# Reading seven latent tiles of the first mixer's input from a second, feature-major copy of x

## The chip, the cores and the metric

The kernel runs on one core of a Trainium2 chip. The metric is the device time of one execution in microseconds (us). The engines are named as in the profile: PE is TensorE (its weight loads are the separate row PEld), DVE is VectorE, ACT is ScalarE, POOL is GpSimd, and SP is SyncE, whose queue issues nearly all DMA transfers of this kernel.

## The reference, cut to what matters

The program is a two-layer trunk of a generator over 1024 latent tokens and 256 context tokens with 1024 features. Layer 0 mixes by windowed attention, layer 1 by gated linear attention; each is followed by an MLP. The change touches only the input of layer 0's mixer: a norm over each token's features, then a scale and a shift per feature, then the projection to q, k and v.

```
def rms_norm(x, gain):
    xf = x.astype(jnp.float32)
    y = xf * lax.rsqrt(jnp.mean(xf * xf, axis=-1, keepdims=True) + NORM_EPS)
    return (y * gain.astype(jnp.float32)).astype(x.dtype)

def modulate(x, gain, shift, scale):
    return rms_norm(x, gain) * (1 + scale) + shift
...
        h_lat = modulate(x_lat, g_pre_mix[i], m_lat[0], m_lat[1])
        h_ctx = modulate(x_ctx, g_pre_mix[i], m_ctx[0], m_ctx[1])
...
    def project(h):
        T = h.shape[1]
        qkv = h @ w_qkv
```

The norm's factor is one number per token; gain, scale and shift are one number per feature. The shifts and scales are themselves a product of the condition vector with `w_mod`.

## The kernel before, in words

**Tiles.** Tokens are cut into ten tiles of 128: tiles 0 and 1 are context, 2 to 9 latent. A tile of rows has tokens on the 128 partitions and 1024 features along them. The projection needs the other layout, features on partitions, since PE contracts over partitions: eight blocks of 128 features by 128 tokens. Every product is made from fp32 numbers split into a high and a low part (`split`, L212 on ACT and L213 on DVE), in three matmuls (`mm3`, L228 to L230). One token tile takes 8 blocks times 3 column groups times 3 = 72 matmuls into q (two groups, one PSUM pair) and kv (one group).

**From rows to operands.** `x_in` (L482) loads a tile of rows by SP's queue. `normed` squares and sums it on ACT (`rms`, L235), makes the factor in two small POOL steps (`rstd`, L241 and L242) and scales the rows on DVE (L430). `modulated` transposes the eight blocks on PE (L442), which land in two PSUM banks of four blocks, applies scale and shift block by block on ACT (L461, even blocks) and DVE (L463, odd blocks) while copying to SBUF, and splits each half into the operands `ah` and `al`. After the matmuls `qkv_out` copies q (L606) and kv (L610) out of PSUM on ACT, `rotary` turns them on DVE and POOL, and `q_out` (L615) stores q to DRAM by SP's queue.

**Order of the work.** `first_tiles` handles the two context tiles while the weights arrive; at its last block (`k == KT - 1`) it calls `pre(2)`, which makes the operands of tile 2 and, like every `pre(i)`, loads the rows of tile i + 2. Rows of tiles 2 and 3 are loaded at block 5 of that loop. Up to here the code stands in a region in which every engine takes its instructions in the order in which they are written. Behind it the tile framework's planner orders each engine's instructions by its own simulated times, and each engine then executes them strictly in that order, SP's queue too: a DMA that waits for its data holds back all that stand behind it. In this part tiles 2 to 6 go through the loop with `qkv_tile`, and tiles 7 to 9 through `qkv_apart`, where PE's order alone is written out and carries pieces of the context tiles' attention (L827 to L854) and, at place 11, the transposes of the next tile. Between the blocks of tiles 2 to 5, `next(mods)` does one step of the sums for later modulation vectors: a load of `w_mod` (L297), a multiply-add on DVE (L308, L310) and, at a vector's end, small PE matmuls (L326). A finished vector goes to DRAM (L335) and comes back as a column per feature (L348, used in L349). After tile 9 the latent attention begins, then the output projection and the MLP.

**Buffers.** One pool of 45 SBUF slots of 4 KB per partition (`u`) serves weights, rows, operands, q and kv; a load waits until a slot is free. PSUM gives four banks (`ps1`) and two bank pairs (`ps2`).

Of the kernel before, what the change touches and what calls it, by code (L numbers as in the profile page):

```python
# [11 lines left out]
F32 = mybir.dt.float32  # L12
F32R = mybir.dt.float32r
AF = mybir.ActivationFunctionType
ALU = mybir.AluOpType
# [3 lines left out]
P = 128  # L19
D = 1024  # L20
KT = D // P
SEQ = 1024
CTX = 256
NC_T = CTX // P
NL_T = SEQ // P
NT = NC_T + NL_T
# [138 lines left out]
class Backbone:  # L165
# [267 lines left out]
    def modulated(self, xn, l, which, s, dst=(), put=None):  # L433

        nc = self.nc
        G, S = self.pre[l, which]
        pts = {}

        def turn(q):
            for k in range(4):  # L440
                kk = 4 * q + k
                nc.tensor.transpose(pts[q][:, P * k : P * (k + 1)], xn[:, P * kk : P * (kk + 1)], self.ident)  # L442

        if self.tight:
            both = self.ps2("xt")
            for q in range(2):
                pts[q] = both[:, 512 * q : 512 * (q + 1)]
                turn(q)
        for q in range(2):
            if not self.tight:  # L450
                pts[q] = self.ps1("xt")
                turn(q)
            pt = pts[q]
            h = None if put else self.half("h").rearrange("p (k t) -> p k t", k=4)
            for k in range(4):
                kk = 4 * q + k
                to = put(kk) if put else h[:, k, :]
                src = pt[:, P * k : P * (k + 1)]
                sc, sh = G[:, s, kk : kk + 1], S[:, s, kk : kk + 1]
                if k % 2 == 0:  # L460
                    nc.scalar.activation(to, src, AF.Identity, scale=sc, bias=sh)  # L461
                else:
                    nc.vector.tensor_scalar(to, src, sc, sh, ALU.mult, ALU.add)  # L463
            for k0, k1, hi, lo in dst:
                a, b = max(k0, 4 * q), min(k1, 4 * q + 4)
                if a < b:
                    self.split(h[:, a - 4 * q : b - 4 * q, :], hi[:, a - k0 : b - k0, :], lo[:, a - k0 : b - k0, :])

    def post_norm(self, y, x, grow):

        nc = self.nc
        r = self.rms(y, self.junk)
        o = self.u(s="xo")
        nc.vector.tensor_tensor(o, y, grow, op=ALU.mult)
        nc.vector.scalar_tensor_tensor(o, o, r, x, ALU.mult, ALU.add)
        return o
# [984 lines left out]
    def gla_running(self, head, g, logs):  # L1461
# [5 lines left out]
        for d, lg in enumerate(logs):  # L1467
            run = self.half("run")[:, :w]
            r3 = run.rearrange("p (c t) -> p c t", t=P)
            l3 = lg.rearrange("p (c t) -> p c t", t=P)  # L1470
            tot, mid = self.tot[head][:, d, self.chunks(g)], self.mid[head][:, d, self.chunks(g)]
            if d == 0:
                nc.vector.tensor_tensor_scan(run, self.reset[:, :w], lg, 0.0, ALU.mult, ALU.add)
                nc.vector.tensor_copy(mid, r3[:, :, 63])
                nc.vector.tensor_copy(tot, r3[:, :, P - 1])
            else:
                nc.vector.memset(run[:, 0:1], 0.0)
                nc.vector.tensor_tensor_scan(
                    run[:, 1:w], lg[:, 0 : w - 1], self.reset[:, 1:w], 0.0, ALU.add, ALU.mult
                )  # L1480
                nc.vector.tensor_copy(mid, r3[:, :, 64])
                nc.vector.tensor_tensor(tot, r3[:, :, P - 1], l3[:, :, P - 1], op=ALU.add)
            nc.vector.tensor_tensor(r3, r3, mid.unsqueeze(2).to_broadcast([P, nch, P]), op=ALU.subtract)
            if g > 0 or d == 0:
                ex = self.u((P, 2, 512), s="ex")
            up, down = (ex[:, 0, :], ex[:, 1, :]) if g else (None, ex[:, d, :w])
            sgn = 1.0 if d == 0 else -1.0
            nc.scalar.activation(down, run, AF.Exp, scale=-sgn / TAU)
            if g > 0:
                nc.scalar.activation(up, run, AF.Exp, scale=sgn / TAU)  # L1490
            res.append((up, down))
# [189 lines left out]
    def run(self):  # L1681
        nc, t = self.nc, self.t
        self.gm, self.pre = {}, {}
        self.q, self.oT = {}, {}
        groups = [[0, 1], [2, 3, 4, 5], [6, 7, 8, 9]]


# [1 line left out]
        h = Acts(self, [[0, 1]])  # L1689

        def pre(i):
            h = Acts(self, [[i]])
            dst = h.pieces(i)
            xn = self.normed(xs.pop(0), dst[0][2])
            self.modulated(xn, 0, 0, self.stream(i), dst)
            if i + 2 < NT:
                xs.append(self.x_in(i + 2))
            return h

        with self.tc.manual_schedule():  # L1700
            self.consts()
            xs = self.xs
            pq, pkv, h = self.first_tiles(xs, h, pre)
# [21 lines left out]
        for i in range(2, NT - 3):  # L1725
            nxt = pre(i + 1)
            does = {k: lambda: next(mods) for k in (0, 2, 5)} if i < NT - 4 else {}
            if i == 4:
                self.kc = [self.u((P, KVH, CTX), F32R, s="kc") for _ in range(2)]
                for k, fs in ((3, self.keys(0)), (4, self.keys(1)), (6, self.queries(self.qs, 0, 0))):  # L1730
                    does[k] = lambda fs=fs: [f() for f in fs]
            self.qkv_tile(i, h, lambda k: does.get(k, int)())
            h = nxt
            self.rotary(i)
            self.q_out(i)
        ctx = self.ctx_rounds()
        with self.tc.manual_schedule(engines={mybir.EngineType.PE}):
            for i in range(NT - 3, NT):
                does = {}
                for n in (1, 5, 9, 13, 17, 21):  # L1740
                    if ctx:
                        does[n] = [ctx.pop(0) for _ in range(2 if (i, n) == (NT - 1, 17) else 1)]
                if i + 1 < NT:
                    nxt = Acts(self, [[i + 1]])
                    dst = nxt.pieces(i + 1)
                    xn = self.normed(xs.pop(0), dst[0][2])
                    if i + 3 < NT:
                        xs.append(self.x_in(i + 3))
                    does.setdefault(11, []).append(lambda: self.modulated(xn, 0, 0, self.stream(i + 1), dst))
                else:  # L1750
                    ks = {}

                    def begin():
                        ks["a"], ks["b"] = self.lat_keys()
                        self.q_back(NC_T)
                        ks["a"][0](), ks["b"][0]()

                    does.setdefault(7, []).append(begin)
                    does.setdefault(11, []).append(lambda: ks["a"][1]())
                    does.setdefault(12, []).append(lambda: (ks["b"][1](), ks["a"][2](), ks["a"][3]()))  # L1760
                    does.setdefault(14, []).append(
                        lambda: [f() for f in self.queries(self.qs, NC_T, 0) + ks["b"][2:4]]
                    )
                    for n in (19, 24):
                        does.setdefault(n, []).append(lambda: next(latents))
                self.qkv_apart(i, h, i < NT - 1, does)
                h = nxt
                if i < NT - 2:
                    self.rotary(i)
                    self.q_out(i)  # L1770
            assert not ctx
# [327 lines left out]
```

## Time and profile before

| | |
|---|---|
| median of three runs | 2597.32 us (2594.55 to 2599.63) |
| the profiled execution's own time | 2597.13 us |
| its span | 2595.4 us |
| matmuls on PE in all | 13451 |
| transposes of L442 in this stage | 64 (63.8 to 204.1 us), eight for each of tiles 2 to 9 |
| data moved by DMA in all | 351.36 MB, 135 GB/s on average |

How to read the lines that the prediction quotes. A line of the timeline gives the start and the length in us from the span's start, the engine (SPq is SP's queue), the kernel's line, the operation, what it writes and reads, shapes, how many were merged into the line, and in brackets how long the engine had stood idle and what released it. A line of the waits gives who waited for whom, the total in us, the times and the longest. A line of the groups gives busy us in all and the mean ns of one, then the idle time before it. Matmuls overlap, so their lengths say less than the distance between two starts.

### The profile page before, as it was taken

How to read it: one execution, taken by the hardware profiler on the slowest of the kernel's cores; microseconds unless marked ns; L12 is line 12 of the kernel's file. 1: busy time of each engine (PE TensorE's matmuls, PEld its weight loads, DVE VectorE, ACT ScalarE, POOL GpSimd, SP SyncE). 2: the span in 40 equal slices, each digit the busy share in tenths (PEclk: the TensorE clock that was granted, in tenths of full speed). 3: DMA queues.
4: the chain of work that ended last, by engine and by line, in shares of the span. 5: the costliest groups of instructions: out<-in, count | busy, mean ns of one | idle time of the engine just before them, and what ended most of it. 6: DMA issues, size and time to landing. Idle time of an engine off the chain costs nothing. (4 is left out here: it accounts for less than half of the span.)

```text
span 2595.4 us, 36179 instructions
## 1 busy us (share of the span) xinstructions
PE 2529.4 (97%) x13451; PEld 2105.8 (81%) x13451; DVE 1703.1 (66%) x2587; ACT 1255.6 (48%) x2350; POOL 435.2 (17%) x720
## 2 busy tenths in 40 slices
PE   7999999999999999999999999999999999999998
PEld 6778888788888888888877888888887888878886
DVE  4775888657766665858777635646658656566676
ACT  3345777644645454433435545334436555545333
POOL 0354666421000000000002213312310000000002
PEclk9999999999999999999999999999999999999999
DMA  9210121322455675737255331103331544567474
GB/s 313 90 66 25 34 59 51 99 89 78 146 157 164 187 224 161 274 130 277 80 173 200 101 91 49 33 18 97 112 103 46 191 142 156 167 244 238 159 232 159
DMA packets 240801, 351.36 MB, mean 135 GB/s; under 512 B 35000, under 2 KB 133584, under 8 KB 240624
## 3 DMA queue, kind: packets, MB, share of 16 engines
q1 hardware_dynamic: 238032, 339.60, 40.4%
q0 software_dynamic: 2592, 9.44, 0.9%
q8 instruction: 106, 1.74, 0.3%
q14 instruction: 71, 0.58, 0.1%
HBM read 273.41 MB, written 75.56 MB: 134 GB/s over the span
## 5 line engine op out<-in xcount | busy, mean ns | idle before, releaser
L229 PE MATMUL p<-ol,oh 128*128 128x512 f32 x896 | 349.8, 390 | 0.2
L230 PE MATMUL p<-oh,ol 128*128 128x512 f32 x896 | 346.5, 390 | 0.0
L228 PE MATMUL p<-oh 128*128 128x512 f32 x896 | 329.3, 392 | 8.6 <-ACT oh L212 5.4
L241 POOL TENSOR_SCALAR rs<-ss 128x1 f32<-128x1 f32 (+1 forms) x78 | 27.7, 355 | 1627.1 <-ACT later L235 1446.4
L213 DVE TENSOR_TENSOR ol<-wh,oh 128x1024 fp32r<-128x1024 f32 x128 | 153.8, 1221 | 81.8 <-ACT oh L212 80.5
L228 PEld LDWEIGHTS p<-oh 128*128 128x128 f32 x896 | 168.3, 188 | 47.0 <-ACT oh L212 8.6
L212 ACT CAST oh<-wh 128x1024 fp32r<-128x1024 f32 x128 | 131.5, 1050 | 154.5 <-DVE wh L1216 34.9
L229 PEld LDWEIGHTS p<-ol,oh 128*128 128x128 f32 x896 | 168.6, 188 | 36.4 <-DVE ol L213 1.5
L230 PEld LDWEIGHTS p<-oh,ol 128*128 128x128 f32 x896 | 168.5, 188 | 35.1
L310 DVE SCALAR_TENSOR_TENSOR ma<-wm,cT,ma 128x1024 f32<-128x1024 f32 x112 | 147.6, 1346 | 40.8 <-DMA wm<-in_w_mod 40.6
L212 ACT CAST oh<-k 128x1024 fp32r<-128x1024 f32 x96 | 98.0, 1055 | 128.1 <-DMA k<-in_w_mlp_out 61.7
L213 DVE TENSOR_TENSOR wi<-wi,wi 128x512 fp32r<-128x512 f32 x176 | 116.7, 687 | 49.7 <-ACT wi L212 45.9
L1046 ACT COPY s<-pa 128x512 f32<-128x512 f32 x96 | 56.0, 584 | 175.4 <-PE pa L230 175.3
L771 POOL TENSOR_SCALAR pr<-pr,den 128x640 f32<-128x640 f32 (+2 forms) x160 | 126.3, 803 | 33.4 <-DVE den L769 21.7
L213 DVE TENSOR_TENSOR ol<-k,oh 128x1024 fp32r<-128x1024 f32 x96 | 113.7, 1220 | 23.6 <-ACT oh L212 20.1
L212 ACT CAST wi<-wi 128x512 fp32r<-128x512 f32 x176 | 103.9, 615 | 33.9 <-DMA hd<-h 15.1
L228 PE MATMUL y<-woh,oh 128*128 128x512 f32 x288 | 115.0, 400 | 2.5 <-ACT woh L212 1.3
L759 ACT ACTIVATE pr<-pr,nm 128x640 f32<-128x640 f32 (+1 forms) x128 | 102.5, 802 | 28.3 <-DVE nm L754 26.9
L230 PE MATMUL y<-woh,ol 128*128 128x512 f32 x288 | 113.2, 394 | 1.3 <-DVE ol L213 1.3
L229 PE MATMUL y<-wol,oh 128*128 128x512 f32 x288 | 112.6, 392 | 0.1
L230 PE MATMUL rp<-wgh,al 128*128 128x512 f32 x288 | 112.0, 390 | 0.0
L229 PE MATMUL rp<-wgl,ah 128*128 128x512 f32 x288 | 112.0, 390 | 0.0
(385 smaller groups left out, 6696.5 us busy)
## 6 DMA issues: line engine op xcount, KB each, us to landing
wm<-in_w_mod SPq DMA_DIRECT2D x96, 512.0 KB
hd<-h SPq DMA_DIRECT2D x80, 512.0 KB
wh<-hd SPq DMA_DIRECT2D x144, 256.0 KB
wh<-in_w_mlp_out SPq DMA_DIRECT2D x144, 256.0 KB
wi<-in_w_mlp_in SPq DMA_DIRECT2D x64, 512.0 KB
k<-hd SPq DMA_DIRECT2D x80, 256.0 KB
k<-in_w_mlp_out SPq DMA_DIRECT2D x80, 256.0 KB
x<-in_x SPq DMA_DIRECT2D x16, 512.0 KB
```

The costliest lines, as they stand in the source:

```text
L212: self.nc.scalar.copy(hi, src)
L213: self.nc.vector.tensor_tensor(lo, src, hi.bitcast(F32), op=ALU.subtract)
L228: mm(out, a[0], b[0], start=start, stop=False, skip_group_check=onto)
L229: mm(out, a[0], b[1], start=False, stop=False, skip_group_check=onto)
L230: mm(out, a[1], b[0], start=False, stop=stop, skip_group_check=onto)
L241: nc.gpsimd.tensor_scalar(r, ss, inv_n, EPS, ALU.mult, ALU.add)
L310: nc.vector.scalar_tensor_tensor(acc[s], raw, c, acc[s], ALU.mult, ALU.add)
L759: nc.scalar.activation(pr, pr, AF.Exp, bias=nm[:, e : e + 1], scale=-1.0, accum_out=sums[:, e : e + 1])
L771: nc.gpsimd.tensor_scalar(pr, pr, den[:, e : e + 1], 0.0, ALU.mult, ALU.add)
L1046: nc.scalar.copy(s["s", j], s["pa"])
```

## The change

The host adds one more input, `in_x_t`: for each of the eight latent tiles the same numbers with features on partitions (partition, feature block, token). The latent tiles 3 to 9 no longer go through `normed` and `modulated` here. Their rows are still loaded, but only for `row_scale`: sum of squares, factor, then the 128 factors are written to a DRAM tile by SP and read back by SP so that every partition holds all 128 of them (`rb`). `xt_in` loads the turned tile, and `from_turned` multiplies it on DVE by the factors (two instructions of four blocks), applies scale and shift in SBUF on ACT and DVE in turn, and splits the halves as before. Tile 2 keeps the old way. `ahead(i)` replaces the load of rows i + 2: it issues the turned tile i + 1 and the rows and factor of tile i + 2 (for i = 2 first the factor of tile 3). In the three tiles with PE's order written out, `from_turned` is called at place 11, where the transposes were.

```
+    def row_scale(self, i, x):
+        r = self.rms(x, x)
+        d = self.dp.tile([P], F32, name=self.nm("rd"))
+        self.nc.sync.dma_start(d.rearrange("(p o) -> p o", o=1), r)
+        self.rb[i] = self.sm.tile([P, P], F32, tag="rb", name=self.nm("rb"), bufs=3)
+        self.nc.sync.dma_start(self.rb[i], d.partition_broadcast(P))
+
+    def xt_in(self, i):
+        self.xt[i] = self.u((P, KT, P), s="xt")
+        self.nc.sync.dma_start(self.xt[i], self.t["x_t"][i - NC_T])
+
+    def from_turned(self, i, dst):
+        nc = self.nc
+        xt, r = self.xt.pop(i), self.rb.pop(i)
+        G, S = self.pre[0, 0]
+        for q in range(2):
+            ks = slice(4 * q, 4 * q + 4)
+            nc.vector.tensor_tensor(xt[:, ks, :], xt[:, ks, :], r.unsqueeze(1).to_broadcast([P, 4, P]), op=ALU.mult)
+            for k in range(4 * q, 4 * q + 4):
+                x, sc, sh = xt[:, k, :], G[:, 0, k : k + 1], S[:, 0, k : k + 1]
+                if k % 2 == 0:
+                    nc.scalar.activation(x, x, AF.Identity, scale=sc, bias=sh)
+                else:
+                    nc.vector.tensor_scalar(x, x, sc, sh, ALU.mult, ALU.add)
+            for k0, k1, hi, lo in dst:
+                a, b = max(k0, 4 * q), min(k1, 4 * q + 4)
+                self.split(xt[:, a:b, :], hi[:, a - k0 : b - k0, :], lo[:, a - k0 : b - k0, :])
...
         def pre(i):
             h = Acts(self, [[i]])
             dst = h.pieces(i)
-            xn = self.normed(xs.pop(0), dst[0][2])
-            self.modulated(xn, 0, 0, self.stream(i), dst)
+            if i == NC_T:
+                xn = self.normed(xs.pop(0), dst[0][2])
+                self.modulated(xn, 0, 0, self.stream(i), dst)
+            else:
+                self.from_turned(i, dst)
+            ahead(i)
+            return h
+
+        def ahead(i):
+
+            if i == NC_T:
+                self.row_scale(i + 1, xs.pop(0))
+            if i + 1 < NT:
+                self.xt_in(i + 1)
             if i + 2 < NT:
-                xs.append(self.x_in(i + 2))
-            return h
+                self.row_scale(i + 2, self.x_in(i + 2))
...
                     nxt = Acts(self, [[i + 1]])
                     dst = nxt.pieces(i + 1)
-                    xn = self.normed(xs.pop(0), dst[0][2])
-                    if i + 3 < NT:
-                        xs.append(self.x_in(i + 3))
-                    does.setdefault(11, []).append(lambda: self.modulated(xn, 0, 0, self.stream(i + 1), dst))
+                    ahead(i + 1)
+                    does.setdefault(11, []).append(lambda: self.from_turned(i + 1, dst))
...
+    arrays["in_x_t"] = np.ascontiguousarray(inputs["x"][0].reshape(NL_T, P, KT, P).transpose(0, 3, 2, 1))
```

More of the change, by code (lines that the diff above doesn't have):

```diff
@@ L1683, in run @@
         self.gm, self.pre = {}, {}
-        self.q, self.oT = {}, {}
+        self.q, self.oT, self.xt, self.rb = {}, {}, {}, {}
         groups = [[0, 1], [2, 3, 4, 5], [6, 7, 8, 9]]
```

## Prediction

> **What bounds the kernel now.** First the page's top and busy times, then the busy time by stretch, then the list of what TensorE waited for between 64 and 215 us, then the timeline at the places that list names.
>
> ```profile
> span 2595.4 us, 36179 instructions
> PE 2529.4 (97%) x13451; PEld 2105.8 (81%) x13451; DVE 1703.1 (66%) x2587; ACT 1255.6 (48%) x2350; POOL 435.2 (17%) x720
> 60.00:220.00 160.00, 152.77 (x779) 123.99 (x780) 114.53 (x157) 64.60 (x153) 74.86 (x100) 0.98 0.22 75
> 220.00:530.00 310.00, 302.02 (x2716) 257.16 (x2715) 231.12 (x483) 219.39 (x561) 177.40 (x331) 0.99 0.20 56
> PE xt L442 <- DVE x L430: 3.3, 1, 3.3
> PE sc L827 <- ACT pr L835: 1.7, 1, 1.7
> PE q L228 <- ACT q L606: 1.4, 1, 1.4
> ```
>
> TensorE (PE) is busy 97% of the span. In the stretch that the change touches (60 to 220 us; columns: length, PE, weight loads, DVE, ACT, POOL busy, granted clock, DMA share, GB/s) it stands 7.2 us of 160. Three named waits stand out there, and the longest, 3.3 us, is a transpose that waits for the normed rows. So what takes instructions off PE here ends the stage sooner by their issue time, as long as their successors are ready. The next stretch is just as full of PE (302 of 310), so time saved at 220 us should reach the end.
>
> The profiled execution took 2597.13 us by its own time, 1.7 more than its span; the median of the three runs is 2597.32 (2594.55 to 2599.63). I sum against 2597.1. About 0.2%, 5.2 us, is what a measurement of this kernel can tell from no change.
>
> **Removed: 56 transposes.** Each of the seven tiles loses eight matmuls of line 442.
>
> ```profile
> 74.43 1.03 PE L442 MATMUL xt<-ident,x 128*128 128x128 f32 x8
> 75.22 0.48 PE L228 MATMUL kv<-wkvh,ah 128*128 128x512 f32 x1
> 75.53 0.40 PE L229 MATMUL kv<-wkvl,ah 128*128 128x512 f32 x1
> 75.77 0.39 PE L230 MATMUL kv<-wkvh,al 128*128 128x512 f32 x1
> 76.00 0.39 PE L228 MATMUL kv<-wkvh,ah 128*128 128x512 f32 x1
> ```
>
> The first column is the start. Ordinary matmuls follow each other every 0.23 us (75.77 to 76.00). From the first transpose to the second matmul behind it (74.43 to 75.53) is 1.10; less one interval, eight transposes cost 0.87 us. Seven tiles: 6.1 us, all on PE.
>
> **Removed: the wait at one transpose.**
>
> ```profile
> 134.62 0.39 PE L230 MATMUL q<-wqh,al 128*128 128x512 f32 x1
> 138.34 1.76 PE L442 MATMUL xt<-ident,x 128*128 128x128 f32 x8 [3.33 <-DVE x L430]
> 139.75 0.77 PE L228 MATMUL kv<-wkvh,ah 128*128 128x512 f32 x1
> 142.03 0.39 PE L230 MATMUL kv<-wkvh,al 128*128 128x512 f32 x1
> 142.26 0.39 PE L228 MATMUL kv<-wkvh,ah 128*128 128x512 f32 x1
> 140.00:160.00 20.00, 20.00 (x90) 16.49 (x90) 15.31 (x18) 5.94 (x11) 10.01 (x9) 0.95 0.48 168
> ```
>
> PE stood 3.33 us and then ran slowly, which the granted clock of 0.95 shows too: eight transposes in 1.41 us (138.34 to 139.75) instead of 0.79 (74.43 to 75.22), and the five matmuls to 142.03 in 2.28 instead of five times 0.23. The stall's price is 3.33 + 0.62 + 1.13 = 5.1 us. The matmuls behind it (kv) belong to a tile whose operands were ready; only the place of the transposes in PE's order made them wait. With no transpose there, nothing of the new path stands in that place, so I take the 5.1 as gone. What is late next is the operand at a tile's first matmul.
>
> **Work that moves on the other engines.**
>
> ```profile
> L430 DVE TENSOR_SCALAR x<-x,rs 128x1024 f32<-128x1024 f32 x8 | 9.4, 1181 | 3.0 <-DMA wm<-in_w_mod 1.5 <-POOL rs L242 1.5
> L213 DVE TENSOR_TENSOR al<-h,ah 128x512 fp32r<-128x512 f32 x16 | 10.6, 686 | 2.4 <-ACT ah L212 2.3
> L709 DVE TENSOR_TENSOR t<-q,rope 128x512 f32<-128x512 f32 x6 | 6.3, 1054 | 0.5 <-ACT q L606 0.5
> L310 DVE SCALAR_TENSOR_TENSOR ma<-wm,cT,ma 128x1024 f32<-128x1024 f32 x112 | 147.6, 1346 | 40.8 <-DMA wm<-in_w_mod 40.6
> L548 DVE TENSOR_SCALAR h<-xT,G,S 128x256 f32<-128x256 f32 x4 | 1.7, 413 | 0.1
> L461 ACT ACTIVATE h<-xt,S,G 128x128 f32<-128x128 f32 x32 | 13.8, 459 | 50.6 <-PE xt L442 41.3 <-DVE h L463 8.0 <-DVE kv L712 0.8
> L463 DVE TENSOR_SCALAR h<-xt,G,S 128x128 f32<-128x128 f32 x32 | 12.4, 406 | 13.5 <-ACT h L461 13.2
> ```
>
> (Columns: busy in all, mean ns of one, idle before it.) On DVE one scaling of 1181 ns per tile goes and two 128x512 multiplications with two tensors come: 686 ns each by the nearest row, 1054 by the slowest of this size, a rotary one. That is 0.2 to 0.9 us more per tile, at most 6.5 in seven, against 45 us in which DVE stands in this stretch: nothing on the path. The VectorE: DVE Perf Modes page of the Trainium skill (section on why `tensor_tensor` can't do 2×_2P) speaks against the exchange: a two-tensor fp32 operation runs at half the rate of a one-tensor scaling from SBUF. The rows agree in kind, and if DVE set the pace the rule would take back about that 0.2 to 0.9 us per tile. Shift and scale stay eight instructions a tile, now from SBUF; 256 columns cost 413 ns there, so 128 cost no more than the 406 and 459 now, and I take no difference. Their mutual waits (13.2 and 8.0 us) may shrink, which is cover only. Square sums and POOL's two small steps stay, a tile earlier.
>
> DMA gets seven tiles of 512 KB more, 3.7 MB. The DMA share of 0.22 at 75 GB/s leaves room for several times that: nothing. Two row loads now go out at 49.60, just behind the last weight; they will no longer stand there.
>
> ```profile
> 49.12 0.38 SPq L220 DMA_DIRECT2D wqr<-in_attn_w_qkv  x1
> 49.60 0.86 SPq L482 DMA_DIRECT2D x<-in_x  x2
> 56.14 1.05 ACT L212 CAST wqh<-wqr 128x1024 fp32r<-128x1024 f32 x1 [2.54 <-DMA wqr<-in_attn_w_qkv]
> 60.10 0.79 PE L228 MATMUL q<-wqh,ah 128*128 128x512 f32 x1 [2.43 <-ACT ah L212]
> ```
>
> That weight landed seven us after its issue, and PE's 2.43 us at 60.10 hang on it. If the loads behind it slow it, up to those 2.4 us could be won; if the queue is served in order, nothing. I take nothing, since other loads close up behind it, and keep the 2.4 for the low end.
>
> **Added: the way through DRAM.** The factor is written to DRAM and read back to all partitions. No such pair stands in the trace; the nearest one is a modulation vector's:
>
> ```profile
> 980.48 0.54 SPq L335 DMA_DIRECT2D md<-mrow  x2
> 981.97 0.39 SPq L348 DMA_DIRECT2D G<-md  x1
> 984.41 0.17 DVE L349 TENSOR_TENSOR G<-G,bcol 128x8 f32<-128x8 f32 x1 [0.18 <-DMA G<-md]
> x1d<-xo POOLq DMA_DIRECT2D x10, 512.0 KB, 3.1
> ```
>
> 1.5 us from the write's issue to the read's, 3.9 to the use. Between the two SP stands, and everything behind it on SP's queue with it: the next turned tile, the next rows, modulation weights and stores of q. A full tile lands in 3.1. From the Square to the factor the chain takes 2.1 us:
>
> ```profile
> 70.04 1.10 ACT L235 ACTIVATE ah<-x 128x1024 fp32r<-128x1024 f32 x1
> 72.05 0.63 ACT L212 CAST ah<-h 128x512 fp32r<-128x512 f32 x1 [0.48 <-DVE h L463]
> 72.17 0.75 DVE L430 TENSOR_SCALAR x<-x,rs 128x1024 f32<-128x1024 f32 x1 [0.15 <-POOL rs L242]
> 68.36 0.50 PE L228 MATMUL q<-wqh,ah 128*128 128x512 f32 x1 [1.41 <-ACT q L606]
> ```
>
> The DMA: Bandwidth & Descriptors page (specifications table) of the Trainium skill adds that writes below 512 bytes are done as read-modify-write; the factor's are 4 bytes each, and no run here shows what that costs.
>
> The one tight place is the first tile of the new path, tile 3. By the order written in the diff its Square comes after the last cast of tile 2. That cast was at 72.05 with the Square ahead of it; without, about 71. So Square 71.6, factor 73.7, read issued 75.2, turned tile issued 75.7 behind it, landed 78.8. Two multiplications, four scalings on two engines, cast and subtraction (0.69 + 0.9 + 0.62 + 0.69) make the first half ready at about 82. PE comes to it when tile 2's 72 matmuls from 68.36 at 0.23 are through: 84.9. That leaves under 3 us, and two of DVE's modulation steps (1346 ns each, line 310) in front would use them up. Every later tile has its factor and its turned tile a whole tile (16.6 us) ahead.
>
> **Sum.** 6.1 + 5.1 removed; new waits between 0 and 5.1 (a wait at tile 3 as dear as that of 138.34), of which I take the middle, 2.5, because the margin of 3 us is near what two DVE steps cost. Forecast: 2597.1 − 11.2 + 2.5 = 2588.4 us.
>
> **Rivals.**
> - *The wait only moves.* The order on the engines is planned anew after the first tiles, and a wait like that of 138.34 comes back elsewhere, since DVE and POOL are as loaded as before. For it: two other waits, of 1.7 and 1.4 us, stand in the same stretch. Against: PE depended on the normed rows there through the transposes alone. Then 2597.1 − 6.1 = 2591.0, and with tile 3's 2.5 too 2593.5.
> - *Slower: SP's queue brings the operands late.* A factor's write waits in SP's queue for its Square, and a Square stands in ACT's queue behind the copy of q out of PSUM, which waits for PE (190.72, 191.64):
>
> ```profile
> 190.72 1.03 ACT L606 ACTIVATE q<-q 128x1024 f32<-128x1024 f32 x1 [0.89 <-PE q L230]
> 191.64 1.05 ACT L235 ACTIVATE ah<-x 128x1024 fp32r<-128x1024 f32 x1
> SPq L615 <- DVE q L712: 111.5, 6, 42.3
> ```
>
> SP already stands 111.5 us at six stores of q. If turned tiles are issued behind both, tiles come late one after another at 5.1 us each. It decides from three of the seven on (11.2 / 5.1 = 2.2); with four, 2597.1 − 11.2 + 20.4 = 2606.3. Against it: two tiles of lead.
> - *It doesn't reach the end.* The attention that follows waits for something else; then about 2597. Against it: PE's 302 of 310 us.
>
> **How the numbers follow.** Forecast 0.52, wait only moves 0.27, slower by SP 0.14, doesn't reach the end 0.07. Forecast and the lower edge of the second rival are faster by over 0.2%: 0.52 + 0.05. Within 0.2%: 0.22 + 0.07. Slower 0.14. The forecast's own range is 2583.5 (2597.1 − 11.2 − 2.4) to 2591 (with all 5.1 of new waits). The whole range goes from that, rounded to 2583, up to 2601, just short of three late tiles (2601.2), and leaves out most of the slow case and a few hundredths below.
>
> **What would show it.** Right: eight transposes of line 442 left before 220 us instead of 64; no PE wait for line 430 after tile 2; the stage's last q copy earlier by 8 to 11 us and the same lead at the end. Wrong: PE waits for `ah` or `al` of a new tile behind the new multiplication, above all near 85 us; or SP standing before a turned tile's load for longer than a tile; or the lead gone between 220 and 530 us.

## The result and the profile after

The changed kernel takes 2635.94 us (median of five runs, 2632.54 to 2638.56) against 2597.32: 1.0146 times as long (95% interval 1.0132 to 1.016). Its profiled execution took 2637.8 us, with a span of 2636.1, which is 40.7 more than before.

The page's top, then the busy time by stretch (the columns as in the prediction):

```profile
span 2636.1 us, 36127 instructions
PE 2528.5 (96%) x13395; PEld 2102.9 (80%) x13395; DVE 1699.2 (64%) x2594; ACT 1255.3 (48%) x2350; POOL 443.2 (17%) x720
```

```profile
60.00:220.00 160.00, 108.82 (x445) 84.23 (x445) 84.60 (x123) 43.85 (x88) 60.46 (x55) 0.84 0.39 107
220.00:530.00 310.00, 301.56 (x2643) 258.88 (x2644) 230.50 (x475) 215.08 (x575) 183.75 (x344) 0.98 0.14 40
200.00:220.00 20.00, 1.65 (x3) 0.83 (x3) 8.86 (x17) 5.37 (x15) 9.05 (x11) 0.50 0.19 68
```

The 56 transposes are gone (13451 matmuls have become 13395). Over the whole span PE now idles 107.6 us (2636.1 − 2528.5), 41.6 more than before. Between 60 and 220 us alone PE stands 51.2 us and not 7.2, which is 44.0 more; the next stretch idles as before, and a little is won back behind it. PE's busy total has fallen by only 0.9 us, although transposes worth 6.1 were removed: what is left runs longer, at a granted clock of 0.84 in the stretch. What PE waited for between 55 and 300 us:

```profile
PE sc L857 <- ACT pr L865: 16.9, 1, 16.9
PE q L230 <- DVE al L213: 10.6, 2, 10.4
PE kt L672 <- POOL k L667: 10.6, 2, 7.4
PE q L228 <- ACT ah L212: 9.8, 3, 6.7
PE q L228 <- ACT q L636: 5.4, 1, 5.4
```

These five lines make 53 us (2.4 of them, at 60.56, stood in the kernel before too), and three different engines are named in them. What holds up all three shows in the list of SP's waits (48 to 280 us) and in SP's own timeline:

```profile
SPq L474 <- POOL rs L242: 63.3, 7, 21.2
SPq L476 <- DMA rd<-rs: 53.5, 7, 8.6
```

```profile
71.25 0.33 SPq L474 DMA_DIRECT2D rd<-rs  x1
79.10 0.33 SPq L476 DMA_DIRECT2D rb<-rd  x1
79.52 0.38 SPq L480 DMA_DIRECT2D xt<-in_x_t  x1
...
90.64 0.33 SPq L474 DMA_DIRECT2D rd<-rs  x1
91.06 0.39 SPq L512 DMA_DIRECT2D x<-in_x  x1
91.54 0.38 SPq L297 DMA_DIRECT2D wm<-in_w_mod  x1
99.72 0.33 SPq L476 DMA_DIRECT2D rb<-rd  x1
```

L474 writes the 128 factors of a tile, 4 bytes from each partition; L476 reads them back and has to wait until the write is confirmed. That took 7.85 us at 71.25 and 9.08 at 90.64; in all seven tiles it is between 7.5 and 9.1. SP stands through it, and everything behind it on its queue too: tile 3's turned copy is not issued before 79.52. The loads that were issued behind the second write, ahead of the read, fare no better. The busy time by stretch, finer (last column: GB/s):

```profile
73.00:79.00 6.00, 6.00 (x28) 4.98 (x27) 0.00 (x0) 0.10 (x1) 0.00 (x0) 1.00 0.00 0
94.00:96.00 2.00, 2.00 (x11) 1.62 (x10) 0.00 (x0) 0.00 (x0) 0.00 (x0) 1.00 0.61 37
98.00:99.70 1.70, 1.70 (x9) 1.43 (x8) 0.00 (x0) 0.00 (x0) 0.00 (x0) 1.00 0.36 19
102.00:104.00 2.00, 2.00 (x10) 1.65 (x10) 0.09 (x1) 1.27 (x3) 0.03 (x1) 1.00 0.85 279
```

During the first write nothing else moves (0 GB/s), so no other transfer explains the 7.85 us. During the second, loads of 512 KB crawl (37 and 19 GB/s in the two stretches shown), and once it is confirmed they run at 279. How PE comes to feel it, in the timeline:

```profile
86.29 1.29 DVE L488 TENSOR_TENSOR xt<-xt,rb 128x512 f32<-128x512 f32 x2 [16.31 <-DMA xt<-in_x_t]
87.02 1.65 ACT L492 ACTIVATE xt<-xt,S,G 128x128 f32<-128x128 f32 x4 [13.93 <-DVE xt L488]
90.27 0.80 PE L228 MATMUL q<-wqh,ah 128*128 128x512 f32 x1 [6.67 <-ACT ah L212]
91.29 0.63 PE L230 MATMUL q<-wqh,al 128*128 128x512 f32 x1
91.72 0.63 PE L228 MATMUL q<-wqh,ah 128*128 128x512 f32 x1
...
102.73 1.06 ACT L235 ACTIVATE x<-x 128x1024 f32<-128x1024 f32 x1 [12.00 <-DMA x<-in_x]
103.92 1.42 DVE L308 TENSOR_SCALAR ma<-wm,cT 128x1024 f32<-128x1024 f32 x2 [12.37 <-DMA wm<-in_w_mod]
118.23 1.28 DVE L310 SCALAR_TENSOR_TENSOR ma<-wm,cT,ma 128x1024 f32<-128x1024 f32 x1 [5.43 <-DMA wm<-in_w_mod]
119.44 0.69 DVE L213 TENSOR_TENSOR al<-xt,ah 128x512 fp32r<-128x512 f32 x1
120.18 0.79 PE L230 MATMUL q<-wqh,al 128*128 128x512 f32 x1 [10.39 <-DVE al L213]
```

At 86.29 DVE multiplies tile 3 after standing 16.31 us for the turned copy, and PE has stood 6.67 when it starts at 90.27. At 120.18 PE stands 10.39 us for a subtraction on DVE whose inputs were there; a modulation step ahead of it on DVE (118.23) had waited for its `w_mod`, which came late. ACT's and POOL's queues jam in the same way behind the Square of the rows (102.73). The longest wait, 16.9 us at 220.88, goes back there too: ACT's scalings of tile 9 waited 14.63 us for DVE's multiplication, and that had waited 8.69 for the turned copy. Behind a stall PE also runs at half speed: from 91.29 to 91.72 a matmul takes 0.43 us in place of 0.23, as it does from 90.27 to 93.00. The Trainium skill (TensorE: Matmul & The Clock Gate, Part 1) says that PE falls to half its clock after being idle and needs some 3.4 us of work to come back; the rows agree in kind, with 2.7 us here.

### The profile page after: what moved, and what is told of

Same layout as the page of the kernel before. It is cut to its first block, busy times and chain, and to the rows that moved or that the text cites. A ratio compares the mean times of both kernels' runs of the same rounds, so it can differ in the third digit from the quotient of the medians.

```text
span 2636.1 us, 36127 instructions
## 1 busy us (share of the span) xinstructions
PE 2528.5 (96%) x13395; PEld 2102.9 (80%) x13395; DVE 1699.2 (64%) x2594; ACT 1255.3 (48%) x2350; POOL 443.2 (17%) x720
## 5 line engine op out<-in xcount | busy, mean ns | idle before, releaser
L212 ACT CAST oh<-k 128x1024 fp32r<-128x1024 f32 x96 | 98.1, 1054 | 127.3 <-DMA k<-in_w_mlp_out 52.0
```

The lines of the kernel that those rows point to most:

```text
L212: self.nc.scalar.copy(hi, src)
```

## The experiments

The theory from the trace: the write of 4-byte pieces costs the time, by being slow to confirm; SP and the loads behind it pay. The rivals: the new path costs it even without the trip through DRAM (more work on DVE, operands late by the order of the queues); or SP stands because it waits for the factor; or it is the number of pieces, 128, and not their size. Times below are medians; ratios are to runs of the kernel before on the same chip, whose medians were 2593.4 to 2596.0 us, with the 95% interval.

**e1: the factors as one piece.** PE turns the column of factors into a row, ACT copies it, and 512 bytes go out from one partition.

```
+        pr = self.ps1("rt")
+        self.nc.tensor.transpose(pr[:1, :P], r, self.ident)
+        row = self.sm.tile([1, P], F32, tag="rrow", name=self.nm("rrow"), bufs=2)
+        self.nc.scalar.copy(row, pr[:1, :P])
-        self.nc.sync.dma_start(d.rearrange("(p o) -> p o", o=1), r)
+        self.nc.sync.dma_start(d.rearrange("(o p) -> o p", o=1), row)
```

> The 128 factors of a tile are first turned into one row by a PE transpose and a small ACT copy, and written to DRAM as one piece of 512 bytes instead of 128 pieces of 4. The read back and all else stay. Theory (the 4-byte write is slow and SP stands for it): SP's wait between write and read falls from about 7.6 us to 1.5 to 2 for each tile, 53.5 us in all to under 15, and the kernel comes down from 2636 to between 2588 and 2605. Rival A (any trip through DRAM is too long, its size doesn't matter): SP's wait stays above 40 us in all and the time within 10 us of 2636. Rival B (the planner's new order is at fault, not the trip): SP's wait falls but the time stays near 2636.

2604.02 us, 1.0026 (1.0015 to 1.0036). SP's timeline, and PE's at the same time:

```profile
72.40 0.25 SPq L478 DMA_DIRECT2D rd<-rrow  x1
73.49 0.33 SPq L480 DMA_DIRECT2D rb<-rd  x1
```

```profile
71.71 0.37 PE L474 MATMUL rt<-ident,rs 128*1 128x128 f32 x1 [6.80 <-POOL rs L242]
```

From write to read it is 1.09 us in place of 7.85, and 31 of the 38 us of loss are gone by the ratios. What is left belongs partly to the experiment: tile 3's small transpose stands in the part whose order is written out, ahead of the last matmuls of the context tiles, and PE stood 6.80 us at it.

**e2: no trip.** The rows are loaded and the factors computed, but nothing is written or read; ones stand in for the factors.

```
         r = self.rms(x, x)
-        d = self.dp.tile([P], F32, name=self.nm("rd"))
-        self.nc.sync.dma_start(d.rearrange("(p o) -> p o", o=1), r)
-        self.rb[i] = self.sm.tile([P, P], F32, tag="rb", name=self.nm("rb"), bufs=3)
-        self.nc.sync.dma_start(self.rb[i], d.partition_broadcast(P))
+        self.rb[i] = self.ones128
```

> The factor is computed as before but neither written nor read: the turned tiles are multiplied by ones, so the norm's factor is left out of seven tiles' input. Rows, squares and POOL steps stay. Theory: without the trip the loss goes and what the change was to gain shows, 2585 to 2595. Rival C (the rows' way through load, Square and POOL holds ACT's and POOL's queues whatever the trip does): stays above 2610. Rival B: near 2636.

2582.46 us, 0.994 (0.9921 to 0.9958): 13.4 us faster than before. Without the trip, and with nothing that waits for a factor, some 53 us are gone (1.0146 less 0.994 of 2597), which is more than the loss; the work on DVE does not carry it.

**e3: the read issued one tile later,** so that SP need not stand between write and read.

```
+        if i + 1 < NT:
+            self.factor_in(i + 1)
+        if x is not None:
+            self.row_scale(i + 2, x)
```

> The factor's read back is issued one tile later than its write, behind the next tile's loads, so SP need not stand for the write. The 4-byte write itself stays. If the standing of SP's queue is the larger part of the loss: SP's wait for the write falls below 20 us in all and the time to 2600 to 2615. If the write also holds the DMA engines for the loads behind it, x and the turned tile still land 8 us or more after their issue and the time stays above 2615.

2623.25 us, 1.0097 (1.0076 to 1.0118).

```profile
SPq L478 <- DMA rd<-rs: 45.6, 7, 7.8
```

The planner put the read close behind the write again, and SP still stood 45.6 us (53.5 before the edit). The edit did not do what it was made for, so over the whole stage it does not tell SP's standing from the slow loads. At the first write it shows the slow loads by themselves: the rows are issued at 73.00, right behind the write of 72.11, and the Square that needs them starts 11.5 us later. The kernel still is some 13 us faster than the changed one.

```profile
84.47 1.06 ACT L235 ACTIVATE x<-x 128x1024 f32<-128x1024 f32 x1 [10.52 <-DMA x<-in_x]
```

**e4: the writes alone, in the kernel before.** The old kernel writes its seven factors to DRAM, 4 bytes a piece, and nobody reads them.

```
+            d = self.dp.tile([P], F32, name=self.nm("rd"))
+            nc.sync.dma_start(d.rearrange("(p o) -> p o", o=1), r)
```

> The kernel before, with the seven factors also written to DRAM as 128 pieces of 4 bytes each, and read by nobody: nothing waits for them. If the write is only slow for whoever waits for it, the time is that of before within 5 us (2592 to 2602). If it holds the DMA engines, loads issued just behind it (the multipliers' w_mod tiles) land about 5 us later than in the kernel before, and the time rises by 0 to 10 us, since PE doesn't wait for these loads there.

2601.93 us, 1.0023 (1.0012 to 1.0034): 6 us, though nothing waits to see the writes confirmed. One line of the kernel before, then e4's timeline and its stretches:

```profile
50.54 3.49 SPq L297 DMA_DIRECT2D wm<-in_w_mod  x4
```

```profile
72.08 0.33 SPq L433 DMA_DIRECT2D rd<-rs  x1
72.97 8.97 SPq L298 DMA_DIRECT2D wm<-in_w_mod  x4
86.71 1.62 DVE L309 TENSOR_SCALAR ma<-wm,cT 128x1024 f32<-128x1024 f32 x2 [7.92 <-DMA wm<-in_w_mod]
```

```profile
80.00:82.00 2.00, 2.00 (x10) 1.67 (x9) 0.00 (x0) 0.00 (x0) 0.00 (x0) 1.00 0.43 37
82.00:84.00 2.00, 2.00 (x10) 1.65 (x10) 0.00 (x0) 0.00 (x0) 0.00 (x0) 1.00 0.95 346
```

Until 82 us, 10 after the write's issue, the loads behind it crawl at 37 GB/s; then they run at 346. So a write of small pieces also holds up transfers that have nothing to do with it. The edit does a second thing, though: the write waits in SP's queue for its factor, so the four loads of `w_mod` behind it go out from 72.97 on and not at 50.54. The 6 us belong to both together. The rest of the loss needs the reader. SP stood 80.9 us waiting for factors here, more than the 63.3 of the changed kernel, which speaks against that standing as the cause of the 38 us.

**e5: no DRAM at all.** DVE puts the factors on a diagonal, one PE matmul with ones spreads them over all partitions, and ACT copies them out of PSUM.

```
+        dg = self.sm.tile([P, P], F32, tag="dg", name=self.nm("dg"), bufs=2)
+        self.nc.vector.tensor_scalar(dg, self.ident, r, None, ALU.mult)
+        pr = self.ps1("rt")
+        self.nc.tensor.matmul(pr[:, :P], self.ones128, dg, start=True, stop=True)
+        self.nc.scalar.copy(self.rb[i], pr[:, :P])
```

> The factor never leaves the chip: DVE makes a diagonal of the 128 factors, one PE matmul with ones on the other side spreads it to all partitions, ACT copies it to SBUF. One matmul, one DVE and one ACT step of 128 columns per tile take the place of write and read. Theory: SP stands no more; seven small matmuls give back under 2 us of the transposes' 6; the time is 2586 to 2597. Rival B (the planner's order is at fault): 2610 or more.

2600.06 us, 1.0022 (1.0012 to 1.0032). No better than e1, though no transfer of the factor is left. PE stands 3.5 us for the copy of q at 68.09 (1.4 at 68.36 before), 4.8 us for `ah` and `al` of tiles 3 and 4 (84.36 to 106.15), whose factors stand in the written order, and 3.9 us at a later tile (144.76 and 148.81).

**e6: no rows at all.** Rows of tiles 3 to 9 are neither loaded nor squared, and ones stand in for the factors.

```
-        r = self.rms(x, x)
...
+        self.rb[i] = self.ones128
```

> Leaves out the rows altogether for seven tiles: no row loads, no Square, no factor (ones in its place). Only the turned tiles, their multiplications, scale and shift stay. This is the bound of what the change could gain: if my sum of the removed work was right (6.1 us of transposes and 5.1 of the wait), 2583 to 2590; if the removed wait comes back elsewhere, 2590 to 2594.

2580.73 us, 0.995 (0.9936 to 0.9964): 12.7 us faster than before. The last copy of kv in this stage comes 13.5 us earlier, at 233.63 against 247.12 in the kernel before:

```profile
233.63 0.59 ACT L638 COPY kv<-kv 128x512 f32<-128x512 f32 x1 [1.66 <-PE kv L230]
```

By the medians that is no more than e2 gained, so loading the rows and making the factors cost nothing that the times show. The traces leave room for a few us: e2's last copy comes at 238.65.

**e7, e8, e9: the first factors behind the written order.** In e5, e1 and the changed kernel, `ahead` for tile 2 moves behind the region in which the order of the code is binding.

```
         def pre(i):
...
-            ahead(i)
+                ahead(i)
...
+        ahead(NC_T)
```

> The kernel with the PE-spread factor, with the first rows' factors (tiles 3 and 4) and loads called after the region of written order instead of inside it, so that the planner may place them. In the run with the spread factor the wait for ah and al of tiles 3 and 4 and slow starts held PE; if the written order of tile 4's row and factor was the cause, 2584 to 2592 and faster than before; if not, within 5 us of 2600.

> The kernel with the one-row write, with the same shift out of the region of written order. PE's wait of 6.8 us for tile 3's factor at the small transpose, which stands in PE's written order ahead of the last context matmuls, should go: 2590 to 2598, if it is that wait; within 4 us of 2604 if not.

> The changed kernel itself, 4-byte write and all, with the same shift. If the written order of the first two factors were a large part of the loss, it comes down by 15 us or more; by the theory of the write, whose 7.6 us stay for every tile, it stays between 2622 and 2640.

| kernel | time, us | ratio | without the move |
|---|---|---|---|
| e7, spread by PE | 2590.03 | 0.9983 (0.9974 to 0.9991) | 1.0022 |
| e8, one piece | 2590.59 | 0.9987 (0.9978 to 0.9996) | 1.0026 |
| e9, 4-byte pieces | 2625.41 | 1.0127 (1.0112 to 1.0143) | 1.0146 |

With the move, e7 and e8 are slightly faster than the kernel before, by 4.5 and 3.9 us (where in the span, the next section says); it was worth some 10 us in both, where an instruction of PE stood in the written order. In the changed kernel, which has none there, the intervals with and without overlap, and SP's wait stays:

```profile
SPq L476 <- DMA rd<-rs: 46.5, 7, 7.6
```

**e10: 128 pieces of 512 bytes.** DVE spreads each factor over 128 columns, and all 128 partitions are written; the read takes the first row. The place in the order is that of the changed kernel.

```
+        self.nc.vector.tensor_scalar(wide, self.ones128, r, None, ALU.mult)
+        d = self.dp.tile([P, P], F32, name=self.nm("rd"))
+        self.nc.sync.dma_start(d, wide)
...
+        self.nc.sync.dma_start(self.rb[i], d[0, :].partition_broadcast(P))
```

> The changed kernel, but each factor is first spread on DVE over 128 columns and written as 128 pieces of 512 bytes (64 KB instead of 512 bytes); the read back takes the first row, so every token gets its tile's first factor. If the size of the piece makes the write slow: SP's wait between write and read falls from 7.6 to about 2 us and the time to 2600 to 2612, as with one row. If the number of pieces does: the wait stays at 6 us or more and the time above 2625.

2590.52 us, 0.9989 (0.9979 to 0.9998). SP's waits, then its timeline:

```profile
SPq L478 <- DVE wide L476: 44.5, 6, 21.7
SPq L480 <- DMA rd<-wide: 12.4, 6, 5.9
```

```profile
111.76 0.33 SPq L478 DMA_DIRECT2D rd<-wide  x1
112.18 0.38 SPq L516 DMA_DIRECT2D x<-in_x  x1
...
113.61 0.38 SPq L480 DMA_DIRECT2D rb<-rd  x1
```

As many pieces as in the changed kernel and 128 times the bytes, yet five of the seven writes are through in 1.5 to 1.9 us (the others in 3.3 and 6.4), and the kernel is slightly faster than before. The number of pieces is not the cause; by the ratios, writing the same number of larger pieces takes away some 41 us (1.0146 less 0.9989), the whole loss. SP stands 44.5 us for the factors here, so that standing does not make the kernel slower than before. Whether it has a part in the 13 us that e2 is faster still is not shown.

**e11: factors three tiles ahead.** e7 with the rows of tiles 5 to 9 loaded and their factors made one tile earlier still.

```
+            if i + 3 < NT:
+                self.row_scale(i + 3, self.x_in(i + 3))
```

> The kernel with the PE-spread factor, free of the written order, with rows and factors loaded three tiles ahead instead of two. If the waits for ah and al that are left (some 9 us of PE idle with the slow starts) come from late factors: 2582 to 2588; if they come from DVE's and ACT's order, as the timeline has it, within 3 us of 2590.

2590.91 us, 0.9987 (0.9978 to 0.9996): the same as e7. Late factors of these tiles are not what keeps e7 behind e6.

**e12: 128 pieces of 256 bytes.** e10 with half the columns; each half of a tile's tokens gets one token's factor.

```
+        d = self.dp.tile([P, 64], F32, name=self.nm("rd"))
+        self.nc.sync.dma_start(d, wide[:, :64])
...
+        self.nc.sync.dma_start(self.rb[i], d[0:2, :].rearrange("a b -> (a b)").partition_broadcast(P))
```

> As e10 (the factor spread over columns and written as 128 pieces, a row read back), with pieces of 256 bytes in place of 512; the read takes the first two of them. Theory A, the price of the write has its edge at 512 bytes: the seven writes again take SP 5 us or more each in place of e10's 1.5 to 1.9, and the time is over 2615 us. Theory B, the price falls steadily with the size of the piece, so that 256 bytes are already far from 4: SP's wait for the write is below 3 us in most tiles and the time stays within 5 us of e10's 2590.5 us.

2591.29 us, 0.9982 (0.9972 to 0.9992).

```profile
112.54 0.33 SPq L478 DMA_DIRECT2D rd<-wide  x1
...
114.38 0.38 SPq L480 DMA_DIRECT2D rb<-rd  x1
```

No slower than with 512 bytes (1.84 us here, 1.85 there). No edge of the price shows between 256 and 512 bytes.

## Why the prediction was wrong, point by point

**The step that failed** is the price of the added trip: "1.5 us from the write's issue to the read's". It was taken from a modulation vector, which goes out in pieces of 2 KB, half a row each, and the factors go out as 4 bytes from each of 128 partitions. Measured: 7.5 to 9.1 us, with everything behind it slowed as well. One piece (e1) takes 1.1 us and 128 pieces of 256 or 512 bytes mostly 1.4 to 1.9, so the row I used was right for the way, and wrong for the size of the piece. I had even given the rule that bears on it: the Trainium skill (DMA: Bandwidth & Descriptors, specifications table) has writes below 512 bytes done as read-modify-write. The runs agree with it in that small pieces are dear, but show no border at 512: 256 bytes were as fast (e12). The range held no such price: I gave the write the one value of the row at hand, with no other end.

**Tile 3.** I had its read issued at 75.2, the turned tile at 75.7, the first half ready at 82 and PE there at 84.9. The factor was there earlier than I said (the write went out at 71.25), but the read went out at 79.10, the turned tile at 79.52, and PE waited until 90.27. A delay of 6.4 us in the write used up the margin of 3 us twice. A second term was too small as well: the turned tile took 6.8 us from its issue to the multiplication that waited for it (79.52 to 86.29), where I had 3.1. Even behind the quick write of e1 it took 5.5 (73.91 to 79.43). The 3.1 was the row of a store by POOL's queue, not of a load.

**"Every later tile has its factor and its turned tile a whole tile ahead"** failed with it. A lead of one tile, 16.6 us, was to cover one trip. It had to cover a write, loads that crawl for its whole length, and queues served strictly in order: a late row stops ACT, a late `w_mod` stops DVE, and either holds back operands of another tile that would have been ready.

**The slower rival**, SP's queue bringing operands late, is what happened, at 0.14 where it should have had more. Its price, 5.1 us a tile from one stall of the kernel before, was too small (38.6 us in all), and its cause was another: not the write that waits for its Square (63.3 us of that in the changed kernel, but 60.3 in e1, which lost 31 us less, and 44.5 in e10, which lost nothing) but the time until the write is confirmed.

**What was removed** was sized about right, but that the end times came so near is in part luck. 6.1 + 5.1 = 11.2 us stood in the sum; without the trip, 13.4 (e2) and 12.7 (e6) came to the end. The last copy of kv in this stage, in the kernel before, e2 and e7:

```profile
247.12 0.59 ACT L610 COPY kv<-kv 128x512 f32<-128x512 f32 x1 [1.67 <-PE kv L230]
238.65 0.59 ACT L639 COPY kv<-kv 128x512 f32<-128x512 f32 x1 [1.67 <-PE kv L230]
248.81 0.59 ACT L644 COPY kv<-kv 128x512 f32<-128x512 f32 x1 [1.66 <-PE kv L230]
```

At that point e2 leads by 8.5 us and e6 by 13.5, around the 11.2. From there to its end the kernel before takes 2348.3 us (2595.4 − 247.12), and every other profiled execution 2338 to 2343, e4 too, whose code is unchanged there. So in these single executions some 5 to 11 us of lead appear behind the stage; the sum has no term for them, and no run here gives their cause. The whole gain of e7 and e8 is of this kind: in the stage e7 is 1.7 us later than the kernel before, and e8 is level with it (247.12).

Eight transposes of line 442 were left, no wait for line 430 came back after tile 2, and the next stretch stayed as full as before. DVE's exchange cost nothing that shows: the multiplications took 785 ns each, inside the 686 to 1054 taken for them. The scalings from SBUF took 414 and 483 ns, against 406 and 459. The 2.4 us at the last weight were not won (PE stood 2.37 us there), as I had taken.

**What stays open.** How the loss divides between SP's standing for the confirmation and the slow loads was not separated: e3 failed at it, and the 6 us of e4 hold a later issue of the loads too. Whether the 4-byte write is slow for the size of its pieces or because all 128 lie in the same 512 bytes of DRAM was not tried. And some 9 us between the best version with factors (e7) and the one with none (e6), 15 us at the last copy of kv, are not explained: e11 excludes late factors from tile 5 on, and the waits that remain in e7 are many and small (4.0, 2.7, 1.8, 1.6 us).

## What to carry to other kernels

Price a DMA by the shape of its pieces, not by its bytes: 512 bytes written from 128 partitions cost seven times what they cost from one, and the loads queued behind them paid too. To spread a column over the partitions, one small matmul with a diagonal or one row written in a piece took the loss away (e7, 0.9983; e8, 0.9987), provided that it did not stand in a part of the code whose order is binding. Inside the stage neither ended ahead of the kernel before. Where a page's rule bears on an added step and no row shows its price, that step's range must reach past the one row at hand, and the queue behind it is part of the price.

## What the runs showed of the hardware that was not expected

- A write of 128 pieces of 4 bytes took 7.85 us to be confirmed with no other transfer under way (0 GB/s from 73 to 79 us), and loads issued behind two such writes moved at 19 to 39 GB/s (changed kernel, 92 to 99.7 us) and 37 GB/s (e4, 72 to 82 us) until the write was through, at 279 and 346 after it.
- 128 pieces of 256 bytes were as fast as of 512 (1.84 and 1.85 us), though one write in each, behind a burst of other loads, took 6 to 8 us (88.68 to 96.43 in e12).
